# Inverting triangular blocks: products on half of the moving columns

## The chip, the cores and the metric

One core of a Trainium2 chip runs the whole program. TensorE multiplies (a matrix product is a load of weights and a pass of moving columns), VectorE and ScalarE work on the results in PSUM and in SBUF, GpSimd does little here, and SyncE issues the transfers. The metric is device time in microseconds; the time of a kernel is the median of its runs.

## The reference

Two blocks of a hybrid network, each of depth 2, on one sequence of 256 tokens and 1024 features. A layer of the first block is a gated feed-forward, a token mixer and a second feed-forward; the mixer has six gated-delta heads, four attention heads and six mLSTM heads. Shifts, scales and gates come from a product of a vector with `ada_w`. The change is in the gated-delta heads. There a unit lower triangular matrix M is solved for each head and each chunk of 64 tokens:

```
A = jnp.where(strict, jnp.einsum('nbhid,nbhjd->nbhij', kb, k) * decay, 0.0)
M = A + jnp.eye(L, dtype=A.dtype)
u = lax.linalg.triangular_solve(M, v * beta[..., None], left_side=True, lower=True, unit_diagonal=True)
w = lax.linalg.triangular_solve(M, kb * jnp.exp(G)[..., None], left_side=True, lower=True, unit_diagonal=True)
```

All of it is in fp32.

## The kernel before

The large products (the feed-forwards and the projections) split each fp32 operand into a high and a low part of a reduced type (fp32r) and take three products of 128x256 (lines 425 to 427). ScalarE makes the high half of a chunk of weights (line 247), VectorE the low half (line 255). These fill TensorE nearly the whole time.

`mixer1` is the token mixer of the first block; it runs twice, for layer 0 and layer 1. It has a generator of projection chunks (`products`), which write PSUM tiles `pw` and from which VectorE makes the causal convolution (lines 820 and 823), and beside it the chains of the heads. The mixer takes a step of the chains, then now and then a step of the projection. `extra` adds chunks of `ada_w`; VectorE multiplies each in two halves with line 453 (`ada_chunk`).

The order in which each engine gets its instructions is not that of the code: a scheduler in the language sets it, by priorities and by its own idea of how long each instruction takes. Only pinned instructions keep their place.

`gdn_invert` inverts the triangular blocks by doubling. A tile of 128x128 holds two blocks of 64 on its diagonal, that is, two chunks of one head; there are 12 tiles a layer, in three groups of four (called A, B, C below, for i0 = 0, 4, 8). `DT` holds the transposed inverse of diagonal blocks of size b, `D` the inverse. A level l, with b = 2^l and l from 1 to 5, joins blocks of b in pairs, in this order:

- first product (line 1107): for each of the four tiles, weights An, moving columns D, 128 columns, into one PSUM bank `py`
- ScalarE copies half of the columns (the runs of b columns with even number) into `U` (line 1108), whose other columns are zero
- second product (line 1113): weights U, moving columns DT, again 128 columns
- VectorE copies the other half (the runs with odd number) into `DT`, where the mask `up` allows (line 1114)
- VectorE transposes DT into D (line 1097), and the next level begins

The runs are picked by `half`:

```
half = lambda t, r: t.rearrange("p i (n r b) -> p r i n b", r=2, b=b)[:, r]
```

The three groups run as three chains beside four attention heads, woven with the projection. `py` has three PSUM banks and `pw` two. After the inversion come the solution (`gdn_finish`, lines 1135, 1141, 1151), the mLSTM heads (lines 1224 to 1246) and the output product. Line 1529, in a head of the second block, is a 128x128 fp32 product whose moving operand is read in runs of b floats, from b = 1 up, each run followed by one 256 floats further on.

Of the kernel before, what the change touches and what calls it, by code (L numbers as in the profile page):

```python
# [19 lines left out]
D = 1024  # L20
# [289 lines left out]
class Net:  # L310
# [771 lines left out]
    def gdn_invert(self, i0, W, An, D, DT, py):  # L1082


        nc = self.nc
        v, sc, mm = nc.vector, nc.scalar, nc.tensor.matmul
        at = lambda i: An[:, i // 2, (i % 2) * 256:(i % 2) * 256 + P]
        D, DT = D[:, i0:i0 + 4], DT[:, i0:i0 + 4]
        U = W.tile([P, 512], F32, bufs=3, tag="U", name="U").rearrange("p (i c) -> p i c", i=4)
        self.pin(nc.gpsimd.memset(U, 0.0))  # L1090
        self.pin(sc.copy(DT, self.cs("ident")[:, None, :].to_broadcast([P, 4, P])))
        h0 = i0 // 2
        for b in range(2):
            v.copy_predicated(out=DT[:, b:4:2], mask=self.mk("up0")[:, None, :].to_broadcast([P, 2, P]),
                              data=An[:, h0:h0 + 2, b * 256:b * 256 + P])

        back = lambda: v.transpose(D, DT)
        back()
        yield
        for l in range(1, 6):  # L1100
            b = 1 << l
            half = lambda t, r: t.rearrange("p i (n r b) -> p r i n b", r=2, b=b)[:, r]
            mask = lambda n: self.mk(n).rearrange("p (n b) -> p n b", b=b)[:, None].to_broadcast([P, 4, 64 // b, b])
            p = py()
            p4 = p.rearrange("p (i c) -> p i c", i=4)
            for i in range(4):
                mm(p4[:, i], at(i0 + i), D[:, i], start=True, stop=True)  # L1107
            sc.copy(half(U, 0), half(p4, 0))
            yield
            p = py()  # L1110
            p4 = p.rearrange("p (i c) -> p i c", i=4)
            for i in range(4):
                mm(p4[:, i], U[:, i], DT[:, i], start=True, stop=True)  # L1113
            v.copy_predicated(out=half(DT, 1), mask=mask(f"up{l}"), data=half(p4, 1))
            yield
            if l < 5:
                back()
                yield
# [656 lines left out]
```

## Time and profile before

| what | us |
|---|---|
| median of three runs | 2068.09 (2067.46 to 2068.87) |
| profiled execution | 2064.67 |
| span of its profile | 2062.9 |
| TensorE busy in the span | 2011.7 |
| VectorE busy | 1596.4 |
| ScalarE busy | 1160.7 |

The span runs from the first to the last instruction; the execution's own time is a little longer. The median of the runs stands 3.42 us above the profiled execution. In the rows PE is TensorE, PEld its weight load, DVE VectorE, ACT ScalarE. A busy PE means that passes are under way, not that the array is at its peak, since passes overlap.

### The profile page before, as it was taken

The numbers are of one execution on the slowest core, as the hardware profiler recorded it, in microseconds if no ns is written. First come the engines' busy times: TensorE is split into PE (matmuls) and PEld (weight loads), VectorE is DVE, ScalarE is ACT, GpSimd is POOL, SyncE is SP. The second block draws the span as 40 slices with busy tenths as digits, with TensorE's granted clock in tenths as the row PEclk, the third lists the DMA queues.
The fourth block names the chain that finished last, engine by engine and source line by source line (L and its number), as shares of the span: only waits on it lengthen the run. The fifth ranks groups of instructions, "written<-read, shape, count | busy, mean of one in ns | idle before, by whom it ended". The sixth has DMA issues, their size and how long they took to land.

```text
span 2062.9 us, 39007 instructions
## 1 busy us (share of the span) xinstructions
PE 2011.7 (98%) x16076; PEld 1962.6 (95%) x16076; DVE 1596.4 (77%) x3028; ACT 1160.7 (56%) x1918; POOL 10.4 (1%) x18
## 2 busy tenths in 40 slices
PE   8999999999999999999999999999999999999997
PEld 7999989899999999999999999999899999989997
DVE  7877898987778775997886459786877697868775
ACT  4644734674447444735574448564765585648554
POOL 0000000000000000000000000000000000000000
PEclk9999999999999999999999999999999999999999
DMA  9785444478875783433377533434465343336541
GB/s 392 302 340 220 169 144 154 146 265 309 306 266 220 305 314 139 169 129 109 122 268 276 182 128 138 141 124 164 158 224 185 108 166 133 117 123 212 198 164 40
DMA packets 59445, 400.72 MB, mean 194 GB/s; under 512 B 6786, under 2 KB 8450, under 8 KB 12291
## 3 DMA queue, kind: packets, MB, share of 16 engines
q1 hardware_dynamic: 59266, 398.23, 52.9%
q8 instruction: 126, 2.06, 0.4%
q14 instruction: 53, 0.43, 0.1%
HBM read 395.05 MB, written 3.15 MB: 193 GB/s over the span
## 4 chain that ended last, share of the span: by engine, by line
PE 90%; DVE 5%; ACT 3%; issue 1%; DMA 0%; SPq 0%; ACTq 0%; DVEq 0%
PE pw L425 14%; PE pw L427 14%; PE pw L426 14%; PE y L425 6%; PE y L427 6%; PE y L426 6%; PE pw L550 3%; PE pw L551 3%; PE pw L553 3%; PE py L1529 2%; PE py L1113 1%; PE py L1107 1%; PE pw L778 1%; PE pw L780 1%; PE pw L779 1%; PE pz L425 1%
## 5 line engine op out<-in xcount | busy, mean ns | idle before, releaser
L255 DVE TENSOR_TENSOR lo<-raw,hi 128x1024 fp32r<-128x1024 f32 (+1 forms) x588 | 705.8, 1214 | 285.3 <-ACT hi L247 283.3
L247 ACT CAST hi<-raw 128x1024 fp32r<-128x1024 f32 (+1 forms) x588 | 601.6, 1041 | 436.7 <-PE pw L427 307.3
L425 PE MATMUL pw<-xh,hi 128*128 128x256 f32 x2536 | 724.2, 286 | 2.3 <-DVE zo L925 2.3
L427 PE MATMUL pw<-xl,hi 128*128 128x256 f32 x2536 | 720.7, 284 | 0.0
L426 PE MATMUL pw<-xh,lo 128*128 128x256 f32 x2536 | 720.3, 284 | 0.0
L425 PEld LDWEIGHTS pw<-xh,hi 128*128 128x128 f32 x2536 | 485.7, 192 | 4.8 <-DVE zo L925 2.4
L426 PEld LDWEIGHTS pw<-xh,lo 128*128 128x128 f32 x2536 | 485.7, 192 | 0.6
L427 PEld LDWEIGHTS pw<-xl,hi 128*128 128x128 f32 x2536 | 485.7, 192 | 0.5
L425 PE MATMUL y<-hh,hi 128*128 128x256 f32 x1056 | 296.3, 283 | 2.3 <-ACT hh L530 1.8
L426 PE MATMUL y<-hh,lo 128*128 128x256 f32 x1056 | 296.9, 283 | 0.5 <-DVE lo L255 0.5
L427 PE MATMUL y<-hl,hi 128*128 128x256 f32 x1056 | 296.3, 282 | 0.1
L425 PEld LDWEIGHTS y<-hh,hi 128*128 128x128 f32 x1056 | 200.9, 191 | 3.2 <-ACT hh L530 2.2
L426 PEld LDWEIGHTS y<-hh,lo 128*128 128x128 f32 x1056 | 201.6, 191 | 0.7 <-DVE lo L255 0.7
L427 PEld LDWEIGHTS y<-hl,hi 128*128 128x128 f32 x1056 | 201.4, 191 | 0.3 <-DVE hl L531 0.3
L453 DVE CUSTOM_DVE_ANT_0 raw<-raw,cb 128x1024 f32<-128x1024 f32 x144 | 171.7, 1219 | 18.7 <-DMA raw<-ada 12.7
L550 PE MATMUL pw<-xh,hi 128*128 128x256 f32 x464 | 118.3, 290 | 18.4 <-ACT xh L480 15.9
L551 PE MATMUL pw<-xh,lo 128*128 128x256 f32 x464 | 116.8, 288 | 0.0
L550 PEld LDWEIGHTS pw<-xh,hi 128*128 128x128 f32 x464 | 89.5, 197 | 21.6 <-ACT xh L480 18.5
L551 PEld LDWEIGHTS pw<-xh,lo 128*128 128x128 f32 x464 | 89.5, 197 | 0.3 <-DVE lo L255 0.2
L530 ACT CAST hh<-h 128x512 fp32r<-128x512 f32 x66 | 40.9, 620 | 68.6 <-DVE h L594 68.0
L553 PE MATMUL pw<-xl,hi 128*128 128x256 f32 x464 | 77.7, 286 | 0.4 <-DVE xl L484 0.4
L553 PEld LDWEIGHTS pw<-xl,hi 128*128 128x128 f32 x464 | 65.4, 193 | 1.2 <-DVE xl L484 1.2
(450 smaller groups left out, 3029.6 us busy)
## 6 DMA issues: line engine op xcount, KB each, us to landing
raw<-w SPq DMA_DIRECT2D x132, 1024.0 KB, 6.8
raw<-ada SPq DMA_DIRECT2D x72, 1024.0 KB, 4.9
raw<-win SPq DMA_DIRECT2D x62, 1024.0 KB, 4.9
raw<-wup SPq DMA_DIRECT2D x44, 1024.0 KB, 5.1
raw<-wdn SPq DMA_DIRECT2D x22, 1024.0 KB, 4.9
raw<-wo SPq DMA_DIRECT2D x12, 1024.0 KB, 4.9
raw<-wkv SPq DMA_DIRECT2D x8, 1024.0 KB, 4.9
raw<-wout SPq DMA_DIRECT2D x8, 1024.0 KB, 5.0
```

Of the source, the lines that this page charges most:

```text
L247: self.net.pin(self.net.nc.scalar.copy(t[:, :m], self.raw[len(self.parts)]), late)
L255: self.net.pin(self.net.nc.vector.tensor_tensor(out=t[:, :m], in0=self.raw[i], in1=h[:, :m].bitcast(F32), op=ALU.subtract), late)
L425: mm(out, wh, xh, start=start, stop=False)
L426: mm(out, wl, xh, start=False, stop=False)
L427: mm(out, wh, xl, start=False, stop=stop)
L453: i = nc.vector.tensor_tensor_reduce(out=t[:, j * D:(j + 1) * D], in0=t[:, j * D:(j + 1) * D], in1=self.cb, scale=1.0, scalar=0.0, op0=ALU ...
L530: self.pin(self.nc.scalar.copy(hi, src), late)
L550: mm(o, wh, xh[:, k], start=k == 0 and n == 0, stop=False)
L551: mm(o, wl, xh[:, k], start=False, stop=False)
L553: mm(p[:, n * S:(n + 1) * S], wh, xl[:, k], start=False, stop=k == KT - 1 and n == 1)
L778: mm(out, ah, wh, start=k == 0, stop=False)
L1529: mm(p[:, (2 * j + c) * P:(2 * j + c + 1) * P], k, r, start=True, stop=True)
```

## The change

Both products take as moving columns only the runs that are kept afterwards: 64 of the 128 columns, picked by `half` with strides from SBUF. Their results lie side by side in PSUM, 4 x 64 floats, so ScalarE's copy and VectorE's masked copy read adjacent floats; they still write in runs of b with strides. The weights are the same whole 128x128 tiles. The number of products, copies and transpositions is unchanged, and so is every value that is used. Both products are now on one line, 1109, the copy into U is on line 1111 and the masked copy on line 1113; lines after that are one less than before.

```diff
-            p = py()
-            p4 = p.rearrange("p (i c) -> p i c", i=4)
-            for i in range(4):
-                mm(p4[:, i], at(i0 + i), D[:, i], start=True, stop=True)
-            sc.copy(half(U, 0), half(p4, 0))
+            def pair(left, right, r):
+
+                p = py()[:, :256].rearrange("p (i n b) -> p i n b", i=4, b=b)
+                x = half(right, r)
+                for i in range(4):
+                    mm(p[:, i], left(i), x[:, i], start=True, stop=True)
+                return p
+            sc.copy(half(U, 0), pair(lambda i: at(i0 + i), D, 0))
             yield
-            p = py()
-            p4 = p.rearrange("p (i c) -> p i c", i=4)
-            for i in range(4):
-                mm(p4[:, i], U[:, i], DT[:, i], start=True, stop=True)
-            v.copy_predicated(out=half(DT, 1), mask=mask(f"up{l}"), data=half(p4, 1))
+            v.copy_predicated(out=half(DT, 1), mask=mask(f"up{l}"), data=pair(lambda i: U[:, i], DT, 1))
             yield
```

The scheduler orders the two mixers anew from the inversion on; the rest of the program keeps its order. Two places in layer 0 follow. The first is TensorE's queue around the third level. U_3208, U_3220 and U_3273 belong to the groups A, B and C; py_3505 is A's second product of level 3, py_3511 and py_3532 are B's first and second of level 3, py_3538 and py_3597 C's, py_3590 and py_3613 A's of level 4; pw_3708 is a projection. Before:

```order
L1113 MATMUL py_3505<-DT_3206,U_3208 128x128 x4
L1107 MATMUL py_3511<-D_3207,An_2733 128x128 x4
L425 MATMUL pw_3708<-xh_2469,hi_3557 128x256
L426 MATMUL pw_3708<-xh_2469,lo_3559 128x256
L427 MATMUL pw_3708<-xl_2470,hi_3557 128x256
L425 MATMUL pw_3708<-xh_2469,hi_3557 128x256
L1113 MATMUL py_3532<-DT_3206,U_3220 128x128 x4
L1107 MATMUL py_3538<-D_3207,An_2733 128x128 x4
L1107 MATMUL py_3590<-D_3207,An_2733 128x128 x4
L1113 MATMUL py_3597<-DT_3206,U_3273 128x128 x4
```

The same place now:

```order
L1109 MATMUL py_3505<-DT_3206,U_3208 128x64 x4
L1109 MATMUL py_3511<-D_3207,An_2733 128x64 x4
L1109 MATMUL py_3532<-DT_3206,U_3220 128x64 x4
L1109 MATMUL py_3538<-D_3207,An_2733 128x64 x4
L425 MATMUL pw_3708<-xh_2469,hi_3557 128x256
L426 MATMUL pw_3708<-xh_2469,lo_3559 128x256
L427 MATMUL pw_3708<-xl_2470,hi_3557 128x256
L425 MATMUL pw_3708<-xh_2469,hi_3557 128x256
L426 MATMUL pw_3708<-xh_2469,lo_3559 128x256
L427 MATMUL pw_3708<-xl_2470,hi_3557 128x256
L1109 MATMUL py_3590<-D_3207,An_2733 128x64 x4
L1109 MATMUL py_3597<-DT_3206,U_3273 128x64 x4
```

The projection products between B's first and second product moved behind C's first product, and there are six of them in place of four.

The second place is VectorE's queue behind the masked copy of py_3505, which the transposition for group A's level 4 follows. Before:

```order
L1114 COPY_PREDICATED DT_3206<-masks1_850,py_3505 128x32x8
L1097 STREAM_TRANSPOSE D_3207<-DT_3206 128x512 x2
L820 SCALAR_TENSOR_TENSOR xm_3654<-pw_3565,small_81,xm_3654 128x254
L1114 COPY_PREDICATED DT_3206<-masks1_850,py_3532 128x32x8
L820 SCALAR_TENSOR_TENSOR xm_3654<-pw_3565,small_81,xm_3654 128x253
L1097 STREAM_TRANSPOSE D_3207<-DT_3206 128x512
```

The same place now:

```order
L1113 COPY_PREDICATED DT_3206<-masks1_850,py_3505 128x32x8
L820 SCALAR_TENSOR_TENSOR xm_3489<-pw_3385,small_81,xm_3489 128x254
L1097 STREAM_TRANSPOSE D_3207<-DT_3206 128x512
L453 ISA raw_3180,ada_973<-raw_3180,cb_100 128x1024
L453 ISA ada_973 128x1
L453 ISA raw_3180,ada_973<-raw_3180,cb_100 128x1024
L453 ISA ada_973 128x1
L820 SCALAR_TENSOR_TENSOR xm_3489<-pw_3385,small_81,xm_3489 128x253
L469 TENSOR_TENSOR ada_973<-ada_973,small_81 128x8
L1097 STREAM_TRANSPOSE D_3207<-DT_3206 128x512
```

The two transpositions that followed the masked copy directly now have both halves of an ada chunk between them; these two stood further ahead in the queue before.

## Rows read from the trace of the kernel before

**Rows 1.** The page: busy time of each engine; share of the chain that ended last.

```profile
PE 2011.7 (98%) x16076; PEld 1962.6 (95%) x16076; DVE 1596.4 (77%) x3028; ACT 1160.7 (56%) x1918; POOL 10.4 (1%) x18
...
PE 90%; DVE 5%; ACT 3%; issue 1%; DMA 0%; SPq 0%; ACTq 0%; DVEq 0%
```

**Rows 2.** Stretches (inversion, then rest of the mixer, per layer): length, busy time, clock, DMA.

```profile
284.00:326.00 42.00, 38.71 (x321) 36.95 (x321) 39.39 (x85) 15.41 (x40) 0.00 (x0) 1.00 0.46 162
326.00:440.00 114.00, 108.23 (x816) 100.12 (x816) 101.40 (x288) 67.98 (x150) 0.74 (x1) 1.00 0.45 155
...
905.00:945.00 40.00, 37.90 (x317) 36.58 (x316) 35.87 (x78) 17.05 (x42) 0.00 (x0) 1.00 0.38 130
945.00:1062.00 117.00, 114.66 (x888) 107.87 (x888) 97.77 (x275) 76.09 (x158) 0.74 (x1) 1.00 0.39 142
```

**Rows 3.** Groups by shape: count, busy us and mean ns, idle before and releaser.

```profile
L1113 PE MATMUL py<-DT,U 128*128 128x128 f32 x240 | 32.2, 280 | 2.2 <-ACT U L1108 1.9
...
L1107 PE MATMUL py<-D,An 128*128 128x128 f32 x240 | 30.9, 276 | 3.2 <-DVE D L1097 2.9 <-DVE ada L469 0.3
```

**Rows 4.** PE in order of time: start us, length us, instruction, count [idle before].

```profile
293.73 2.02 PE L1107 MATMUL py<-D,An 128*128 128x128 f32 x16 [1.45 <-DVE D L1097]
295.59 1.95 PE L1113 MATMUL py<-DT,U 128*128 128x128 f32 x16
```

**Rows 5.** PE in order of time, layer 0, products of 6 and of 64 moving columns.

```profile
347.75 0.37 PE L1226 MATMUL pz<-gl,consts 128*128 128x6 f32 x2
347.98 1.53 PE L1151 MATMUL py<-U,An 128*128 128x64 f32 x12
349.35 0.44 PE L1244 MATMUL pz<-R,consts 128*128 128x128 f32 x2
```

**Rows 6.** PE in order of time, layer 0, products with 64 weight columns.

```profile
339.68 0.91 PE L1135 MATMUL py<-U,An 64*64 64x64 f32 x12
340.52 0.39 PE L425 MATMUL pw<-xh,hi 128*128 128x256 f32 x1
```

**Rows 7.** PE in order of time, line 1529: moving runs of 1, 2, 4 floats.

```profile
1278.30 1.55 PE L1529 MATMUL py<-XQ,km 128*128 128x128 f32 x8
...
1283.04 1.12 PE L1529 MATMUL py<-XQ,km 128*128 128x128 f32 x8
...
1285.74 1.13 PE L1529 MATMUL py<-XQ,km 128*128 128x128 f32 x8
```

**Rows 8.** Waits of PE, 284 to 440 us: total us, times, longest.

```profile
PE py L1107 <- DVE D L1097: 1.4, 1, 1.4
PE py L1113 <- ACT U L1108: 1.4, 3, 0.5
```

**Rows 9.** PE in order of time, layer 1, start of the inversion.

```profile
908.86 1.16 PE L1113 MATMUL py<-DT,U 128*128 128x128 f32 x8 [0.54 <-ACT U L1108]
911.45 2.02 PE L1107 MATMUL py<-D,An 128*128 128x128 f32 x16 [1.43 <-DVE D L1097]
```

**Rows 10.** DVE in order of time, first levels of layer 0.

```profile
289.42 1.18 DVE L453 CUSTOM_DVE_ANT_0 raw<-raw,cb 128x1024 f32<-128x1024 f32 x1
...
292.35 0.71 DVE L1114 COPY_PREDICATED DT<-masks,py 128x256 f32<-128x256 uint8 x1
292.86 1.32 DVE L1097 STREAM_TRANSPOSE D<-DT 128x512 f32<-128x512 f32 x2
```

**Rows 11.** All engines in order of time, third level of layer 0.

```profile
304.07 1.06 PE L1107 MATMUL py<-D,An 128*128 128x128 f32 x8
...
304.44 0.43 DVE L1114 COPY_PREDICATED DT<-masks,py 128x256 f32<-128x256 uint8 x1
304.78 1.30 DVE L1097 STREAM_TRANSPOSE D<-DT 128x512 f32<-128x512 f32 x2
...
305.93 1.16 PE L1113 MATMUL py<-DT,U 128*128 128x128 f32 x8 [0.32 <-ACT U L1108]
306.00 0.45 DVE L820 SCALAR_TENSOR_TENSOR xm<-pw,small,xm 128x254 f32<-128x254 f32 x1
```

## Prediction

> **What bounds the kernel now.** I read the page first, then the stretches by window, then the groups of the two product lines, then the single rows around them. The page says that TensorE is busy for 2011.7 of 2062.9 us and that the chain which ends last runs through it for 90% of the span [rows 1]. So a change of the two products is worth what it takes out of TensorE's time, or out of a wait of TensorE; time that it takes from ScalarE or VectorE counts only where TensorE waits for them. The windows then show where the inversion stands: 284 to 326 us in layer 0 and 905 to 945 us in layer 1. In both the granted clock is 1.00, which is the 2.4 GHz level, and TensorE is idle for 3.3 and 2.1 us of the stretch. VectorE, however, is busy for 39.39 of 42 us in layer 0 [rows 2]. The reader should keep that: whatever VectorE has late there, TensorE may wait for.
>
> The two products are 240 passes each over the kernel [rows 3]. The program has 120 matrix products on each line (4 per step, 3 groups, 5 levels, 2 layers), so a product of 128x128 in fp32 runs as two passes, each with its own weight load. 480 passes are touched in all.
>
> **What halving the columns does to a pass.** Back to back, sixteen passes of 128 moving columns begin 293.73 us and the next line begins 295.59 us: 116 ns a pass [rows 4]. What would 64 columns take? The trace has such a product with the same 128x128 weights, line 1151: twelve passes of 64 columns fill 347.98 to 349.35 us, 114 ns a pass. Just ahead of it line 1226 has only 6 moving columns, and its two passes take 347.75 to 347.98 us, 115 ns each [rows 5]. So 128, 64 and 6 columns cost the same, as long as each pass has 128 columns of weights to load. That it is the weights which set this period, and not fp32 as such, is seen in line 1135: 64 moving columns again, but 64x64 weights, twelve passes in 0.84 us, 70 ns a pass [rows 6]. The edit halves the moving operand and leaves the weights (the block of An, or of U) at 128 columns. By these rows the 480 passes keep their 114 to 116 ns, and the saving on TensorE's stream is 0. The work that hides it is the next pass's weight load.
>
> The Trainium skill, "TensorE: Matmul & The Clock Gate", section "LDWEIGHTS (loading the stationary operand)", says that a load's time goes by the weight columns; its formula, columns over 1.2, gives an estimate of 107 ns for 128, near the 114 and 115 ns measured here at 64 and 6 moving columns. The same page's section "Back-to-back issue gap" lists a gap that falls from about 134 to about 60 cycles between 128 and 64 columns when loads are left out; by that table the sum would be that of the first rival below. The trace sides with the load.
>
> **What it does to the waits.** TensorE waits for the copy into U (line 1108) three times in layer 0, 1.4 us together, and once for 0.5 us in layer 1. It waits for the transposed D once in each layer, 1.4 us each time [rows 8, 9].
>
> The last pass of a product ends sooner with 64 columns. Nothing shows this directly for these shapes; the nearest row is the 70 ns pass, 46 ns less than 116 ns. Four waits for U times 0.05 us is -0.2 us.
>
> The readers of PSUM now read 256 adjacent floats in place of runs of b. The masked copy took 0.71 us at level 1, where runs are of 2 floats [rows 10], and 0.43 us at level 3 [rows 11]. If the strided read of PSUM causes the difference, the change saves 0.28 us on the chain to D at level 1; if the strided write to DT or the mask causes it, nothing. The wait for D stands at that place in both layers, so the bounds are 0 and -0.6 us; I take the middle, -0.3 us. Elsewhere VectorE's copies lie beside TensorE's stream.
>
> **What the new order does.** The scheduler counts the products as shorter and places other work anew, from the inversion to the end of each mixer. In layer 0 it used to put four products of the input projection between the third level's first product of group B and the second (py_3511, py_3532); TensorE still waited 0.32 us for U there [rows 11]. Now nothing stands between, so TensorE meets the whole wait of 0.5 us, as it does in its other waits for U [rows 8]: +0.2 us. The four projection products run elsewhere at their own price.
>
> Six projection products now stand ahead of group A's fourth level (py_3590), and VectorE has both halves of an ada chunk (line 453) between the masked copy of py_3505 and the second transposition after it, which that level needs. On VectorE: the copy begins 304.44 and takes 0.43, then line 820 with 0.45, a transposition with 0.66, two halves of 1.18, line 820 again with 0.45, the transposition with 0.66 [rows 10, 11]; that ends near 309.4 us. On TensorE: py_3511 begins at 304.07 [rows 11], three products of 8 passes at 0.116 us are 2.8 us, the wait 0.5 us, six projection products at the kernel's mean of 2011.7/16076 = 0.125 us are 0.75 us; it arrives near 308.1 us. So a new wait of some 1.3 us. Behind it in TensorE's queue stand both second products of that round and the next projection products, so all of it is lost. Without line 453 there it would be none; bounds 0 and +1.3 us, and I take the upper, since the two rows stand in the order. In layer 1 I find no ada chunk at that place and put 0 there, with +1.3 us as a bound.
>
> **The sum.** 0 for the passes, -0.2 and -0.3 us for shorter waits, +0.2 and +1.3 us for the new order: +1.0 us. The profiled execution took 2064.67 us with a span of 2062.9 us, so I expect about 2065.7 us of such an execution. It was 3.42 us below the median of the runs, 2068.09 us, so the median becomes about 2069.1 us. The bounds of the terms give 2067.5 to 2071 us. No change can be told by this measurement under about 0.2%, or 4.1 us: the forecast is "the same".
>
> **Rivals.**
>
> First, the passes go by their moving columns after all. Then 480 passes fall from 114 to 70 ns, -21 us, and the median is near 2048 us. For it: line 1135 runs at such a period. Against it: lines 1151 and 1226, which have the same weights as here. Chance 0.03.
>
> Second, the new order happens to close waits. TensorE is idle for 9.1 us from 284 to 440 us in layer 0, and for 4.4 us from 905 to 1062 us in layer 1 [rows 2], with the same code in slightly different orders. If layer 0 came down to layer 1's idle time, 4.6 us would go, and with the new wait not happening the median would be near 2063.5 us. Chance 0.09.
>
> Third, on the other side: VectorE's queue. The place is the one of the sum: a transposition, or the low half of a weight chunk (line 255), that stands behind ada halves of 1.18 us while TensorE's order already asks for it. VectorE has 2.6 us to spare in the inversion of layer 0 [rows 2]. Each such place costs about 1.3 us; with three more beside the one counted it passes 0.2%, and if layer 1 grew the idle time of layer 0, +4.6 us, the median would be 2073.7 us. Chance 0.10.
>
> Fourth, the strided moving operand is slow to read. Line 1529 shows it: with single floats 8 passes last 1.55 us, with runs of 2 and of 4 they last 1.12 and 1.13 us [rows 7], so 0.42/8 = 0.053 us more a pass. Were the 96 passes of level 1 to pay this, +5.0 us, 2074.1 us; were all 480 to pay, +25 us. Against it: level 1 already has runs of 2, the rows show no price for these, and 64 columns even at 1.55/8/128 us each are 0.097 us, under the 0.114 us of the load. Chance 0.03. The Trainium skill, "SBUF — State Buffer", section "Door 1: The DMA port swizzle", says in its note on cachelines that reads need two hits in a 16-byte line; the rows agree, with 1.55 us for one and 1.12 us for two.
>
> **Chances and range.** The forecast has 0.75. Faster by over 0.2% is the first and second rival, 0.12; slower is the third and fourth, 0.13; the same is 0.75. The range goes from the second rival to the third, with a little for the fourth: 2063.5 to 2074.0 us; what lies outside is mainly the first rival and the dearer half of the fourth.
>
> **What the profile after would show.** Right: the groups of the new product line with 128x64 beside the old mean duration, and rows of eight passes that still begin some 0.11 us apart; TensorE's whole busy time within a few us of 2011.7; the waits for D of level 1 at 1.4 us or slightly less; a wait of about 1.3 us for D near 308 us in layer 0. Wrong: eight passes in about 0.56 us (the first rival), passes of level 1 longer than those of level 5 (the fourth), or windows of the two mixers whose idle time moves by over 4 us while the passes stay as they are (the second and third). I would be wrong in kind, not in size, if the period of a pass turned out to follow moving columns when these are strided.

## The result, and the profile after

The changed kernel takes 2118.82 us (median of 4 runs, 2113.55 to 2126.41), the kernel before 2068.07 us in the same runs: ratio 1.0249, 95% interval 1.0234 to 1.0264. That is 50.75 us slower, where I forecast +1.0 us and a range of 2063.5 to 2074.0 us. The profiled execution took 2113.55 us with a span of 2111.8 us, 48.9 us more than the span before.

The page of the changed kernel, busy time by engine, and TensorE's granted clock in 40 equal slices (9 stands for 0.9 or more):

```profile
PE 2050.9 (97%) x16076; PEld 1999.0 (95%) x16076; DVE 1595.9 (76%) x3028; ACT 1161.1 (55%) x1918; POOL 10.4 (0%) x18
...
PEclk9999989999999999987999999999999999999999
```

TensorE is busy for 2050.9 us, 39.2 us more than before [rows 1], for the same number of passes. Its idle time grew from 51.2 to 60.9 us. So four fifths of the loss are time in which TensorE works. The line of the clock, which on the page of before holds only nines, shows an 8 in the sixth slice and an 8 and a 7 in the eighteenth and nineteenth: the two inversions.

The same stretches as in [rows 2], and within them two that I cut by the clock (columns: stretch, length, busy time of PE, PEld, DVE, ACT and POOL, granted clock, DMA share, GB/s):

```profile
284.00:326.00 42.00, 38.94 (x215) 38.11 (x215) 24.41 (x49) 8.16 (x19) 0.00 (x0) 0.64 0.28 101
296.00:326.00 30.00, 28.96 (x134) 28.59 (x134) 14.72 (x30) 2.72 (x9) 0.00 (x0) 0.50 0.30 106
...
905.00:945.00 40.00, 37.46 (x252) 36.02 (x252) 31.42 (x67) 11.13 (x19) 0.00 (x0) 0.86 0.29 106
934.00:978.00 44.00, 43.29 (x202) 42.80 (x202) 15.30 (x36) 5.22 (x15) 0.00 (x0) 0.50 0.01 4
```

In layer 1 the changed kernel runs some 22 us late, so the stretch from 905 us holds only the start of its inversion. From 296 to 326 us and from 934 to 978 us the granted clock is 0.50, the lower of its two levels (1.2 GHz). TensorE is not idle there: it is busy for 28.96 of 30 us and for 43.29 of 44 us. It issues 134 and 202 passes in that time, 0.216 and 0.214 us each. VectorE, with 39.39 of 42 us the nearly full engine of this stretch before [rows 2], has fallen to 24.41 us: its masked copies now wait 12.9 us there for TensorE's second product, in place of 1.6 us.

TensorE in order of time around the fall and the return of layer 0, and around the fall of layer 1 (start, length, instruction, count, idle before):

```profile
291.17 1.11 PE L1109 MATMUL py<-DT,U 128*128 128x64 f32 x8 [0.58 <-ACT U L1111]
293.72 1.97 PE L1109 MATMUL py<-D,An 128*128 128x64 f32 x16 [1.45 <-DVE D L1097]
295.53 3.42 PE L1109 MATMUL py<-DT,U 128*128 128x64 f32 x16
...
302.93 3.62 PE L1109 MATMUL py<-D,An 128*128 128x64 f32 x16
306.35 3.62 PE L1109 MATMUL py<-DT,U 128*128 128x64 f32 x16
...
326.44 0.30 PE L425 MATMUL pw<-xh,hi 128*128 128x256 f32 x1
326.58 1.00 PE L1109 MATMUL py<-DT,U 128*128 128x64 f32 x8
...
930.60 1.10 PE L1109 MATMUL py<-DT,U 128*128 128x64 f32 x8 [0.58 <-ACT U L1111]
933.15 2.83 PE L1109 MATMUL py<-D,An 128*128 128x64 f32 x16 [1.45 <-DVE D L1097]
```

The sixteen passes at 293.72 us still go at full clock: the next line begins 1.81 us later, 0.113 us a pass (116 ns before [rows 4]). The sixteen at 302.93 us are followed by the next line at 306.35 us: 3.42/16 = 0.214 us. Ahead of the fall TensorE had run products of 64 columns with waits of 0.58 and 1.45 us between them. In layer 1 the fall, at 934 us, stands right behind waits of the same length; until then the narrow passes ran at full clock there too. Such waits stand at the same places in the kernel before (1.45 us in layer 0 [rows 4], 0.54 and 1.43 us in layer 1 [rows 9]), and there the clock stays at 1.00. The clock returns at 326 us, in a row of projection products of 256 columns.

The groups of the new line beside [rows 3], and the waits of TensorE over the whole span:

```profile
L1109 PE MATMUL py<-DT,U 128*128 128x64 f32 x240 | 46.7, 366 | 3.3 <-ACT U L1111 3.1
...
L1109 PE MATMUL py<-D,An 128*128 128x64 f32 x240 | 44.7, 353 | 4.4 <-DVE D L1097 4.4
```

```profile
PE py L688 <- DVE s L684: 4.6, 2, 2.3
PE py L1109 <- DVE D L1097: 4.4, 3, 1.5
PE py L1109 <- ACT U L1111: 3.1, 7, 0.6
```

The mean duration of a pass rose from 280 and 276 ns to 366 and 353 ns. In the two slow stretches stand 288 passes of line 1109 (62 + 56 and 88 + 82 in the groups of these windows) at about 0.213 us in place of 0.113 us, +28.8 us, and 48 projection passes at 0.213 in place of 0.119 us, +4.5 us: 33.3 of the 39.2 us. Shorter falls of the clock near 410 and 1080 us are part of the rest. The waits for D and for U are 2.7 us longer together than before, and the one at line 688, the statistics of the layer norm that follows the mixer, has grown to 4.6 us.

### The profile page after: what moved, and what is told of

Read it like the earlier page. It is cut to its first block, busy times and chain, and to the rows that moved or that the text cites. A ratio compares the mean times of both kernels' runs of the same rounds, so it can differ in the third digit from the quotient of the medians.

```text
span 2111.8 us, 39005 instructions
## 1 busy us (share of the span) xinstructions
PE 2050.9 (97%) x16076; PEld 1999.0 (95%) x16076; DVE 1595.9 (76%) x3028; ACT 1161.1 (55%) x1918; POOL 10.4 (0%) x18
## 4 chain that ended last, share of the span: by engine, by line
PE 88%; DVE 5%; ACT 5%; DMA 1%; issue 1%; SPq 0%; ACTq 0%; DVEq 0%
PE pw L425 14%; PE pw L426 14%; PE pw L427 14%; PE y L425 6%; PE y L427 6%; PE y L426 6%; PE py L1109 4%; PE pw L550 2%; PE pw L551 2%; PE pw L553 2%; PE py L1528 1%; ACT hi L247 1%; DVE lo L255 1%; PE pz L425 1%; PE pz L426 1%
## 5 line engine op out<-in xcount | busy, mean ns | idle before, releaser
L550 PEld LDWEIGHTS pw<-xh,hi 128*128 128x128 f32 x464 | 89.7, 197 | 21.0 <-ACT xh L480 18.4
```

What stands on the lines that cost most here:

```text
L550: mm(o, wh, xh[:, k], start=k == 0 and n == 0, stop=False)
```

## The experiments

Two theories stood at the start. **Columns**: passes of 64 columns behind loads of 128 weight columns keep TensorE's queue full, but make its clock fall. **Order**: the scheduler's new order, with its waits, makes it fall. The diff changes both, and the PSUM layout too, so they had to be parted. In the following kernels the order is fixed first, by letting the scheduler see one column count, and the count in the finished program is then changed (`todo` holds the 120 + 120 products; the traces show the same order on TensorE, VectorE and ScalarE as in the kernel named):

```diff
...
+    for bb in f.blocks:
+        for k, i in enumerate(bb.instructions):
+            if i.name in todo:
+                b, r = todo.pop(i.name)
+                def ap(a):
+                    p, *d = a.ap
...
+                    return a.__replace__(ap=[p] + [(2 * b, 64 // b), (1, b)], offset=a.offset + r * b, bass_ap=None)
+                bb.instructions[k] = i.__replace__(ins=[ap(i.ins[0]), *i.ins[1:]], outs=[ap(i.outs[0])])
```

These write the 64 columns into PSUM at their old places; the readers read runs of b, as before.

**Half of the columns, order before** (the diff above on the kernel before).

> Half of the columns in the order of the kernel before: every engine issues the same instructions in the same order as before, only the 120 + 120 products stream 64 columns in place of 128. Theory columns: the granted clock falls to 0.50 in the dense run of products (293 to 315 us and its like in layer 1), passes go from 0.113 to about 0.213 us there, and 22 to 60 us at half the clock cost 11 to 30 us: 2079 to 2098 us. Theory order: the clock stays at 1.00 and the time at 2064 to 2073 us. Theory both (few columns and the new order together): also 2064 to 2073 us; the next run then parts the two.

Measured: 2108.20 us against 2067.60, ratio 1.0194 (1.0181 to 1.0208): +40.6 us. Its windows:

```profile
284.00:326.00 42.00, 39.34 (x215) 38.55 (x213) 28.32 (x57) 9.61 (x22) 0.00 (x0) 0.63 0.29 100
...
905.00:945.00 40.00, 37.97 (x255) 36.83 (x253) 34.66 (x75) 12.05 (x22) 0.00 (x0) 0.85 0.31 106
```

The clock falls with every instruction where it was, so the new order is not needed for it. In the profiled execution TensorE is busy for 2054.4 us, 42.7 us more than before, and idle for 51.3 us, as before: all of this loss is time in which TensorE works. I had expected 11 to 30 us; the clock stayed low from about 295 to 336 us and from 932 to 981 us, longer than I had allowed for.

**All columns, order after** (scheduled with 64 columns, then given 128).

> All 128 columns in the order of the changed kernel: every engine issues the same instructions in the same order as the changed kernel, only the products stream 128 columns again. Theory columns: the granted clock stays at 1.00 in the inversion, passes stay at 0.113 us, and the time is 2064 to 2075 us, with what the new order's own waits cost or give. Theory order: the clock falls as in the changed kernel, 2110 to 2126 us. Theory both: 2064 to 2075 us with the run before at the same.

Measured: 2083.75 us, ratio 1.0082 (1.0068 to 1.0096): +16.1 us, outside what either theory had. Its windows and its waits:

```profile
284.00:326.00 42.00, 36.62 (x305) 34.87 (x303) 32.34 (x72) 15.02 (x35) 0.00 (x0) 1.00 0.36 126
326.00:440.00 114.00, 106.24 (x738) 95.37 (x737) 97.86 (x276) 59.07 (x137) 0.74 (x1) 0.94 0.43 153
905.00:945.00 40.00, 37.02 (x305) 35.66 (x305) 31.01 (x63) 12.74 (x26) 0.00 (x0) 1.00 0.26 90
```

```profile
PE py L1107 <- DVE D L1097: 4.9, 4, 1.5
PE py L688 <- DVE s L684: 4.6, 2, 2.3
PE py L1113 <- ACT U L1108: 3.3, 7, 0.5
```

In both inversions the clock is 1.00 (in layer 1, where this kernel runs 12 us late, up to 960 us as well), so the big fall needs the 64 columns. But the order has a price of its own: waits, and shorter falls (0.94 on the mean from 326 to 440 us). The profiled execution is the slowest of the four (2087.96 us): its idle time is 12.2 us above that of before and its busy time 11.0 us, at a mean clock of 0.990. The other three ran at 0.994, close to the 0.995 of before, so in them the clock's share is smaller. One place where the order costs, first TensorE, then VectorE:

```profile
433.92 1.21 PE L688 MATMUL py<-s,consts 128*128 128x256 f32 x4 [2.30 <-DVE s L684]
434.93 1.06 PE L688 MATMUL py<-r,consts 128*128 128x256 f32 x2
435.78 1.06 PE L688 MATMUL py<-sq,consts 128*128 128x256 f32 x2
```

```profile
431.99 1.21 DVE L255 TENSOR_TENSOR lo<-raw,hi 128x1024 fp32r<-128x1024 f32 x1
433.12 0.41 DVE L685 TENSOR_TENSOR s<-s,sq 128x256 f32<-128x256 f32 x1
433.45 0.42 DVE L684 TENSOR_TENSOR s<-s,r 128x256 f32<-128x256 f32 x1
```

TensorE has nothing else left at 431.6 us and asks for the statistic s. On VectorE the low half of a weight chunk (line 255, 1.21 us) stands ahead of the last two additions of s. TensorE waits 2.30 us. Its first four passes of line 688 take 1.01 us, the next two 0.85 us, where two took 0.43 us in the kernel before: the clock has fallen again. In the kernel before, the wait at this place was 0.2 us.

**The change without its PSUM layout** (64 columns in both the schedule and the program, PSUM as before).

> The change with one part undone: the products make 64 columns, but write them into PSUM at the places where they stood before, so ScalarE and VectorE read runs of b as before. All engines keep the order of the changed kernel. Theory columns (TensorE streams too few columns per pass, so its clock falls and the weight loads take twice as long) and theory order (the new order alone makes TensorE's clock fall): both 2113 to 2126 us, as the changed kernel, with the granted clock at 0.50 near 296 to 326 us and 935 to 978 us. Theory PSUM (the adjacent layout in PSUM is what costs): 2064 to 2073 us.

Measured: 2114.89 us, ratio 1.0231 (1.0217 to 1.0245): +47.3 us. So the adjacent layout is not what costs. Columns alone +40.6, order alone +16.1, both +47.3: the two overlap. The waits stay nearly whole: in the profiled execution TensorE's idle time is 8.8 us above that of before, against 12.2 us with the order alone. What shrinks is the time at the lower clock: about 31 and 44 us in the two inversions here, 41 and 48 us with the columns alone. Why it is shorter in the new order was not tested.

**The kept columns streamed twice.** The layouts of the change, but 128 moving columns:

```diff
...
+                p4 = p.rearrange("p (i t n b) -> p i t n b", i=4, t=2, b=b)
...
-                    mm(p[:, i], left(i), x[:, i], start=True, stop=True)
-                return p
+                    mm(p4[:, i], left(i), x[:, i, None].to_broadcast([P, 2, 64 // b, b]), start=True, stop=True)
+                return p4[:, :, 0]
```

> The change's layouts, but the 64 kept columns are streamed twice: strided moving operand of 128 columns (64 of them, then the same 64 again), PSUM read as adjacent runs by ScalarE and VectorE, order of all engines as before. Theory columns: clock 1.00, 2064 to 2070 us, no loss from strides; if the adjacent reads of PSUM helped level 1 (my term of -0.3 us), 2067 to 2068 us. Theory strides (strided moving operand or adjacent PSUM cost the time): 2090 to 2126 us.

Measured: 2066.64 us, ratio 0.9996 (0.9987 to 1.0005), in the order of before. Its inversions:

```profile
284.00:326.00 42.00, 38.73 (x321) 36.96 (x320) 39.44 (x84) 14.97 (x39) 0.00 (x0) 1.00 0.46 157
905.00:945.00 40.00, 37.91 (x318) 36.63 (x317) 35.76 (x79) 17.17 (x43) 0.00 (x0) 1.00 0.37 129
```

Strides in the moving operand cost nothing that could be told here, and the adjacent reads of PSUM give nothing that could be told. What differs from the kernel that lost 40.6 us is how many columns each pass streams (and the place in PSUM); the clock stays at 1.00.

**One part alone**, order before: only the first product of each step (the line shown), only the second (`r == 1`), or both in one group of three (`i0 == 4`).

```diff
-    todo = {n: (b, r) for n, b, r in TWO}
+    todo = {n: (b, r) for n, b, r, i0 in TWO if r == 0}
```

> Only the first product of each step streams 64 columns, the second keeps 128; order of all engines as in the kernel before. If the loss goes with the number of passes that are cut, half of the 40.6 us that both cost in this order: about 2088 us. If it is a matter of the clock falling or not, it lies near one of the ends: 2064 to 2072 us with the granted clock at 1.00 in the inversion, or 2095 to 2110 us with it at 0.50 from 296 us on.

> Only the second product of each step streams 64 columns, the first keeps 128; order as before. The first product alone cost 5.6 us, both 40.6 us. If the two halves of the change cost alike, 2070 to 2076 us, far from half of 40.6 us; if all of the loss sits in the second product, 2095 to 2108 us.

> Both products stream 64 columns in one of the three groups (i0 = 4), 128 in the other two; order as before. By the pass count a third of 40.6 us: 2081 us. If the clock stays at 1.00, the rows show what a pass of 64 columns with 128 weight columns takes at full clock beside its neighbours of 128: by my prediction the same 0.114 to 0.116 us, so 2064 to 2070 us; if the pass goes by moving columns, 160 passes at 0.070 us give -7 us, 2061 us.

Measured: the first product +5.6 us (1.0027, 1.0016 to 1.0038), the second -0.5 us (1.0002, 0.9993 to 1.0011), one group +3.3 us (1.0017, 1.0006 to 1.0027). None of the three lies in a range that I had worked out; the nearest bounds are 2072 us (measured 2073.17), 2070 us (2067.28) and 2070 us (2070.85). So 240 narrow passes, half of them, cost 0 to 5.6 us, and all 480 cost 40.6 us: nothing here goes by the count of passes. The windows of the first of these, around the place where the clock fell for good in the others:

```profile
294.00:296.00 2.00, 2.00 (x15) 2.00 (x15) 2.00 (x4) 1.02 (x3) 0.00 (x0) 0.72 0.93 389
296.00:298.00 2.00, 2.00 (x11) 2.00 (x11) 0.55 (x2) 0.78 (x3) 0.00 (x0) 0.50 0.01 4
298.00:300.00 2.00, 2.00 (x18) 1.95 (x17) 1.66 (x2) 0.00 (x0) 0.00 (x0) 0.93 0.03 8
```

The clock falls at about 295 us here too, but comes back by 299 us, among products of 128 columns. Where the others are narrow too, it stays low. Why the first product alone costs something and the second nothing is left open. The group alone gave no clean price of a narrow pass at full clock, since its clock fell for a few us as well.

**Narrow weights in place of narrow moving operands.** Each product in two, with 64 weight columns each and all 128 moving columns. From here on the scheduler orders each kernel anew, so the order is not held:

```diff
-                mm(p4[:, i], at(i0 + i), D[:, i], start=True, stop=True)
+                for r in HALVES:
+                    mm(p4[r, i], at(i0 + i)[:, r], D[:, i], start=True, stop=True)
...
```

> Every product in two, each with 64 weight columns (output rows 0 to 63, then 64 to 127) and all 128 moving columns: 960 passes in place of 480. If the weight load sets the period, a pass takes 0.058 to 0.070 us as in line 1135 and the sum is 56 to 67 us against 55 us: 2068 to 2080 us, with the clock at 1.00, since TensorE streams more columns than before. If 128 moving columns take 0.115 us whatever the weights: 960 x 0.115 = 110 us, 2123 us.

Measured: 2068.49 us, ratio 1.0003 (0.9994 to 1.0013), for 960 passes.

```profile
294.54 1.97 PE L1108 MATMUL py<-D,An 128*64 128x128 f32 x32 [1.45 <-DVE D L1097]
296.31 1.97 PE L1115 MATMUL py<-DT,U 128*64 128x128 f32 x32
```

32 passes of 128 moving columns take 1.77 us, 0.055 us each. With 128 weight columns the same moving operand took 0.116 us [rows 4]. So it was the weight load that set the old period, as the prediction said.

**64x64 blocks.** Up to level 5 only the two diagonal blocks of each matrix are used, by the inversion and by what follows it. This kernel holds D, DT and U as those blocks (masks and the first copies accordingly):

```diff
-                mm(p4[:, i], at(i0 + i), D[:, i], start=True, stop=True)
+                for r in HALVES:
+                    mm(p4[r, i], at(i0 + i, r), D[r, i], start=True, stop=True)
...
-            DT = M.tile([P, 12, P], F32, tag="DT", name="DT")
+            DT = M.tile([P, 24, 64], F32, tag="DT", name="DT")[:, :12]
...
-                    mm(hs(p[r], h), DT[r, 2 * h + t, r], hs(x[r], h), start=True, stop=True)
+                    mm(hs(p[r], h), DT[r, 2 * h + t], hs(x[r], h), start=True, stop=True)
```

> D, DT and U hold only the two 64x64 diagonal blocks of each matrix (no level up to 5 needs more): each product is two of 64 weight columns by 64 moving columns, 960 passes, and ScalarE's and VectorE's copies, masks and transpositions have half of the columns. Theory columns: TensorE streams 64 columns in 0.058 to 0.070 us, as densely as 128 in 0.115 us, so the clock stays at 1.00; passes 0 to +12 us, shorter copies and transpositions take 0 to 5 us out of TensorE's waits: 2063 to 2080 us. If the two halves overlap in the array, down to 960 x 0.035 = 34 us of passes: 2043 us. If the clock falls all the same: 2090 us or more.

Measured: 2055.95 us, ratio 0.9945 (0.9933 to 0.9958): 11.6 us faster than before, and faster than both kernels of this case. It lies between the two cases that I had worked out, 2043 us and 2063 to 2080 us. TensorE in order of time, layer 0, and one of its waits:

```profile
298.38 1.21 PE L1112 MATMUL py<-DT,U 64*64 64x64 f32 x32
299.47 0.68 PE L1106 MATMUL py<-D,An 64*64 64x64 f32 x16
...
304.98 1.15 PE L1112 MATMUL py<-DT,U 64*64 64x64 f32 x32
305.96 0.63 PE L1106 MATMUL py<-D,An 64*64 64x64 f32 x16
```

```profile
PE py L686 <- DVE s L682: 4.0, 2, 2.4
```

32 passes take 1.09 and 0.98 us, 0.034 and 0.031 us each. In line 1135, where all passes of a group sit at one place of the array, the same shape took 0.070 us [rows 6]; here the lower and the upper half alternate. 960 x 0.033 = 32 us in place of 55 us would be 23 us; about half arrives. In the profiled execution TensorE is busy for 2000.5 us, 11.2 us less than before, and idle for 2.6 us more, with the wait shown (the norm's statistics) at 4.0 us in place of 0.2; the mean clock is 0.993 in place of 0.996. How the rest divides was not measured.

The Trainium skill, "TensorE: Matmul & The Clock Gate", section "The mechanism" of its part on packing small matmuls, says that a weight load runs beside a product in flight only when the two use different groups of rows. The trace agrees as far as 64x64 blocks go, with 0.031 to 0.034 us for alternating halves and 0.070 us for one. It does not bear out the "only": with all 128 rows in every pass, 6, 64 and 128 moving columns take the same 0.114 to 0.116 us [rows 4, 5], so the columns there run beside a load of the same rows.

**Where those 11.6 us come from**: the same kernel with each product's 64 columns streamed twice.

```diff
-            p4 = py()[:, :256].rearrange("p (i c) -> p i c", i=4)
+            p5 = py().rearrange("p (i t c) -> p i t c", i=4, t=2)
+            p4 = p5[:, :, 0]
...
-                    mm(p4[r, i], at(i0 + i, r), D[r, i], start=True, stop=True)
+                    mm(p5[r, i], at(i0 + i, r), D[r, i, None].to_broadcast([64, 2, 64]), start=True, stop=True)
...
```

> The kernel with 64x64 blocks, but each product streams its 64 columns twice (128 moving columns): ScalarE and VectorE do the same half work, TensorE's passes take 0.055 us or so as in the kernel with the weights in halves, so 960 x 0.055 = 53 us as before. If the 11.6 us came from shorter passes, the time goes back to 2064 to 2069 us; if it came from the shorter copies, masks and transpositions, it stays at 2054 to 2059 us.

Measured: 2068.68 us, ratio 1.0004 (0.9995 to 1.0013).

```profile
294.72 1.96 PE L1107 MATMUL py<-D,An 64*64 64x128 f32 x32 [0.32 <-DVE D L1096]
296.49 1.94 PE L1114 MATMUL py<-DT,U 64*64 64x128 f32 x32
```

32 passes take 1.77 us again, 0.055 us each, and the gain is gone, though ScalarE and VectorE still do half of the work. In the profiled executions TensorE is busy for 18.4 us more than with the blocks streamed once (2018.9 against 2000.5 us) and idle for 6.9 us less. So it was TensorE's passes; the order differs too, but the idle time that it leaves moved the other way.

**The change of this case, made on the blocks**: 32 of 64 moving columns.

```diff
-            p4 = py()[:, :256].rearrange("p (i c) -> p i c", i=4)
+            p4 = py()[:, :128].rearrange("p (i n b) -> p i n b", i=4, b=b)
...
-                    mm(p4[r, i], at(i0 + i, r), D[r, i], start=True, stop=True)
+                    mm(p4[r, i], at(i0 + i, r), half(D, 0)[r, i], start=True, stop=True)
...
```

> The change of this case, made once more on the kernel with 64x64 blocks: 32 of the 64 moving columns, adjacent in PSUM. There a pass took 0.031 to 0.038 us. If the pass stays at its weight load (64 columns), nothing is saved; theory columns: TensorE streams half of the columns in the same time, the granted clock falls to 0.50 in the inversion, and some 30 us at half the clock cost about 15 us: 2065 to 2080 us. If the clock stays at 1.00, it is 2053 to 2060 us, and halving is then harmless where loads overlap.

Measured: 2082.71 us, ratio 1.0067 (1.0053 to 1.0080): 26.8 us slower than the blocks with all columns. In the profiled executions 24.7 us of this are TensorE's busy time. Its inversions:

```profile
284.00:326.00 42.00, 39.14 (x525) 35.68 (x523) 28.95 (x76) 12.70 (x34) 0.00 (x0) 0.67 0.36 121
905.00:945.00 40.00, 38.65 (x524) 35.32 (x524) 25.14 (x69) 12.17 (x30) 0.00 (x0) 0.71 0.27 95
```

The clock falls again (0.67 and 0.71 on the mean of the two stretches), this time with no wait over 0.42 us in the products ahead, and again right behind such a wait (near 297 and 922 us). The loss was larger than the 2065 to 2080 us that I had worked out.

## Why the prediction was wrong

**What bounds the kernel: right.** The loss is TensorE's time, 39.2 of the 48.9 us of the profiled executions.

**"By these rows the 480 passes keep their 114 to 116 ns, and the saving on TensorE's stream is 0": the step that failed.** The reason behind it held: the weight load sets the period (0.116 us with 128 weight columns, 0.055 us with 64, for the same 128 moving ones), and at full clock a narrow pass takes 0.113 us. But I read the clock of 1.00 in [rows 2] as a property of the stretch, and it was one of the work in it. With all passes narrow, the granted clock went to 0.50 for 30 and 44 us with TensorE busy, and a pass to 0.213 us. The rows from which I took the price of narrow passes, [rows 5] and [rows 6], are groups of 0.8 to 1.4 us beside other work; they show what a pass costs at a given clock, not what a long run of them does to the clock. None of my four rivals let the clock change, so no case of mine reached 2100 us. That the fall needs the narrow columns is shown with the order held: 64 columns in the old order (+40.6 us), the same streamed twice (-1.0 us), and 128 columns in the new order (clock 1.00 in the inversions). The blocks with 32 in place of 64 (+26.8 us) agree, though there the order moved as well. The falls in the inversions all begin right behind waits of TensorE, which alone do not bring them, since the kernel before has such waits too. Whether a run of narrow passes with no wait ahead of it would lose the clock was not tested, and what the chip counts to set its clock, these runs do not show.

The Trainium skill, "TensorE: Matmul & The Clock Gate", section "What's actually happening", says that the default is the lower level and that recent activity releases the clock, with two levels only. The trace agrees with the two levels: stretches lie at 1.00 or at 0.50. The section "HAM oscillation — how this bites in real kernels" tells of idle gaps as the way to lose the clock. Here the fall does stand behind waits (0.58 and 1.45 us), but with 128 columns such waits did not bring it, and it lasted for 30 us in which TensorE was busy for 28.96 us.

**The new order, +0.2 and +1.3 us: mis-sized, and looked for at the wrong place.** By itself it cost 16.1 us. At the place I had worked out, near 308 us, the kernel with all columns and the new order shows this, first on TensorE, then on VectorE:

```profile
307.65 0.39 PE L425 MATMUL pw<-xh,hi 128*128 128x256 f32 x1 [0.72 <-DVE xm L820]
```

```profile
304.86 1.18 DVE L453 CUSTOM_DVE_ANT_0 raw<-raw,cb 128x1024 f32<-128x1024 f32 x1
305.97 1.22 DVE L453 CUSTOM_DVE_ANT_0 raw<-raw,cb 128x1024 f32<-128x1024 f32 x1
...
307.12 0.48 DVE L820 SCALAR_TENSOR_TENSOR xm<-pw,small,xm 128x253 f32<-128x253 f32 x1
```

The two ada halves do stand there, and they make TensorE late. But it waits 0.72 us in place of 1.3 us, and six projection passes earlier than I thought: for line 820, which frees the PSUM tile of the next projection products, not for the transposition. In the changed kernel itself this wait is gone, covered by the slow clock. Most of the price lies where I did not look: of the 12.2 us of idle time that the order adds in the profiled execution, 4.4 us are at line 688 at the ends of both mixers (4.6 us, 0.2 us before), 2.0 us waits for D and 1.4 us waits for U; short falls of the clock come on top. At line 688 it is the mechanism of my third rival, VectorE's queue, for which I had worked out +4.6 us. How the 16.1 us of the median divide between waits and clock was not measured.

**The level-1 copy, -0.3 us: nothing.** In the changed kernel it takes as long with adjacent PSUM as it did with strided [rows 10]:

```profile
292.33 0.71 DVE L1113 COPY_PREDICATED DT<-masks,py 128x256 f32<-128x256 uint8 x1
```

So the strided read of PSUM does not set that time; the strided write to DT and the mask are left, and were not parted. **The shorter tails, -0.2 us: not seen.** The waits for U are 0.52 and 0.58 us where they stand (0.54 us before [rows 9]), and there are seven in place of four.

**The rivals.** The first (passes by moving columns) is out: 0.113 us at full clock. It came true only once the weights were halved: with 64 weight columns, 128 moving columns take 0.055 us, and 64 take 0.031 to 0.034 us where the halves alternate. The second did not happen: TensorE's idle time grew by 9.7 us. The fourth is out: strides cost nothing that could be told, ratio 0.9996.

## What to carry to other kernels

Where the weight load sets a pass's period, narrowing the moving operand saves next to nothing (0.113 against 0.116 us a pass), and a long run of such passes, here behind waits of TensorE, can cost the clock as well; what paid here was blocks of 64 weight and 64 moving columns at alternating halves of the array (-11.6 us), while weights in halves with twice the passes gave nothing (1.0003). Read a price from short groups only as a price at their clock, and ask of a long run what its clock will be; the row of granted clock by window is the one to put beside every duration. When a scheduler counts an edited instruction as shorter, follow the new order to the end of what it moves, not just to the places beside the edit.

## What the hardware showed that I had not expected

TensorE's granted clock fell to 0.50 and stayed there for 30 and 44 us, with TensorE busy for 28.96 and 43.29 us of them and no wait in them over 0.52 us. Narrowing half of the passes cost 5.6 us or nothing, narrowing all cost 40.6 us. Products of 64x64 blocks at alternating halves of the array go at 0.031 to 0.034 us a pass, against 0.070 us at one place. And the changed kernel's runs spread over 12.9 us (2113.55 to 2126.41), those of before over 1.4 us beside them; the shortest had a mean clock of 0.977, the longest 0.969.
